# Attention projections: the transposes of normed query and key tiles stand five half-product steps behind their own product instead of four

## The chip, the cores and the metric

The kernel runs on one core of a Trainium2 chip. The metric is the time of one whole execution on the device, in microseconds (us). Engines are named as the profile names them: PE (TensorE; PEld is its weight load), DVE (VectorE), ACT (ScalarE), POOL (GpSimd), SP (SyncE, which issues most of the DMAs).

## What is computed

Two layers of a decoder with 16 meta tokens ahead of 512 tokens, width 1024. Layer 0 is attention with forget gates, layer 1 a gated recurrence; each is followed by a mixture-of-experts FFN. The change touches only the start of layer 0, where queries and keys are projected, normed for each head of 64 values, and laid out with the head dimension on the partitions:

```python
def fox_attention(h, w_in, b_f, g_q, g_k, w_out):
    q, k, v, f_logit = jnp.split(h @ w_in, [D_MODEL, 2 * D_MODEL, 3 * D_MODEL], axis=-1)
    q = rms_norm(q.reshape(bsz, length, FOX_HEADS, FOX_HEAD_DIM), g_q)
    k = rms_norm(k.reshape(bsz, length, FOX_HEADS, FOX_HEAD_DIM), g_k)
    v = v.reshape(bsz, length, FOX_HEADS, FOX_HEAD_DIM)
    ...  # softmax((q k^T) * scale + forget sums), times v, times w_out
```

## The kernel before

The projection goes by **chunks**: `q` first half, `k` first half, `q` second half, `k` second half, `v` first half, `v` second half (512 columns each; below q0, k0, q1, k1, v0, v1). A chunk has four **products**, one for each 128 tokens. A product is 24 matmuls of 128x512: weights and tokens are each split into a rounded part and a remainder (`whi`, `wlo`, `xhi`, `xlo`), and for each half of the weights come 8 matmuls with `whi` (L340 `pp<-whi,xhi` and `pp<-whi,xlo`) and 4 with `wlo`. The 16 meta rows have a product of their own, `pm` (L357, 8 matmuls), fed from the raw weights when a weight tile of the next chunk is split; that is after the first and after the last product of a chunk.

What follows a product of `q` or `k` is `heads_norm`, in three parts. At the product's end ACT squares it (L419 `sq`) and DVE sums by head (L421). The part `second` takes the root on ACT (L138, L139), refines it on DVE (L157 to L161) and scales the tile (L430 `qn<-pp,rs`). The part `third` transposes `qn` on PE (L438, four transposes into `pq`), and ACT copies `pq` into `qT` or `kT` with the gain (L439).

When the parts are issued is ruled by a counter, `Later`. It ticks twice in a product: after its 13th matmul (the **middle**) and at its end, behind `qk_post`, which calls `heads_norm`. A part put in with `later.at(n, f)` is issued at the n-th tick from then on:

```python
later.at(2, second)
later.at(4, third)
```

So `second` of a product stands in the middle of the next one. The engines' queues are in this order, each engine works its queue in order, and semaphores do the rest. A chunk's end is a busy place: behind the tick stands `W.split`, which feeds the meta product on PE, rounds the next weights on ACT (L280 `whi`) and takes the remainder on POOL or DVE or half on each (L295, L289 `wlo`). The meta rows pass through `heads_norm` too: the sums of their four partial products (L372 `mt`, and `vm` for `v`) and their `second` and `third` are put in with the same counter, in the middle of the next chunk's first product, so that their transposes (L438 from 16 rows) stand beside those of that chunk's first tile.

Buffers that bear on the order: `qn` has two, `sq` one, `pp` three, `pq` shares two PSUM banks with the transposes of the input, and `pm` shares two with small constants. During the chunks DVE also builds small masks (L857 to L867 `lmask`) as the iterator `later.slow`, one piece at each tick.

After the projections come the attention itself (L626 and on), the output projection with the router, and the experts of layer 0, whose weights begin to load when the attention's buffers close.

Of the kernel before, what the change touches and what calls it, by code (L numbers as in the profile page):

```python
# [127 lines left out]
def rsqrt(K, y, x, shape, pool, tag, tables):  # L128


    run(rsqrt_steps(K, y, x, shape, pool, tag, tables))
# [243 lines left out]
def fox(K):  # L375

    nc, tc = K.nc, K.tc
    later = Later()
    with tc.tile_pool(name="ax", bufs=1, reuse_waits="tile") as per:
# [15 lines left out]
        with tc.tile_pool(name="ap", bufs=1, reuse_waits="tile") as mid, \  # L395
# [20 lines left out]
            def heads_norm(src, r, dst, gcol, hp0, c0):  # L416

                sq = wk.tile([128, 512], FT, name="sq", bufs=1)
                nc.scalar.activation(sq[:r], src, AF.Square)  # L419
                ss = wk.tile([128, 8], FT, name="ss")  # L420
                nc.vector.tensor_reduce(ss[:r], sq[:r].rearrange("t (h d) -> t h d", d=HD), axis=AX.X, op=OP.add)  # L421
                nc.vector.tensor_scalar(ss[:r], ss[:r], 1.0 / HD, EPS, op0=OP.mult, op1=OP.add)
                held = []

                def second():
                    rs = wk.tile([128, 8], FT, name="rs")
                    qn = wk.tile([128, 512], FT, name="qn")
                    held.append(qn)
                    rsqrt(K, rs[:r], ss[:r], [r, 8], wk, "hn" if r == 128 else "hm", True)
                    nc.vector.tensor_tensor(qn[:r].rearrange("t (h d) -> t h d", d=HD),  # L430
                                            src.rearrange("t (h d) -> t h d", d=HD),
                                            rs[:r, :, None].to_broadcast([r, 8, HD]), op=OP.mult)

                def third():
                    qn, = held
                    p = ps.tile([128, 4, 128], FT, name="pq", tag="tr")
                    for a in range(4):
                        nc.tensor.transpose(p[:, a, :r], qn[:r, 128 * a:128 * a + 128], K.ident[:r, :r])  # L438
                    nc.scalar.activation(dst[:, hp0:hp0 + 4, c0:c0 + r], p[:, :, :r], AF.Copy, scale=gcol)  # L439

                later.at(2, second)
                later.at(4, third)

            def qk_post(p, i, kind, half):
                dst, gcol = (qT, gq) if kind == "q" else (kT, gk)
                heads_norm(p, 128, dst, gcol, 4 * half, M + 128 * i)

            def meta_done(mr, kind, half):
                if kind == "v":
                    mr.sum(vm[:, 512 * half:512 * half + 512])  # L450
                    return
                mt = wk.tile([M, 512], FT, name="mt", bufs=1)
                mr.sum(mt)
                dst, gcol = (qT, gq) if kind == "q" else (kT, gk)
                heads_norm(mt, M, dst, gcol, 4 * half, 0)
# [1636 lines left out]
```

## Time and profile before

| what | value |
|---|---|
| median of 3 runs | 1759.38 us (1757.03 to 1763.66) |
| the profiled execution, whole time | 1755.66 us |
| its span, first to last instruction | 1753.7 us |
| PE busy | 1617.5 us, 92% of the span |
| DVE, ACT, POOL busy | 758.1, 411.7, 280.3 us |
| mean granted clock of PE | 0.962 of full |

The projections take about the first tenth of the span, 9 to 190 us. PE is the engine that works nearly all the time there, so its idle time in that stretch, and time at a lower granted clock, are what to look for. The rows are quoted below, ahead of the prediction.

### The profile page before, as it was taken

To read this page: it belongs to the slowest core of one execution; us is meant where nothing else is said; L and a number is where in the kernel's file an instruction comes from. 1 tells how busy PE (TensorE), PEld (TensorE's weight loads), DVE (VectorE), ACT (ScalarE), POOL (GpSimd) and SP (SyncE) were. 2 spreads that over 40 slices of the span, in tenths; PEclk is the share of its full clock that TensorE was granted. 3 is DMA by queue.
4 is the path that set the end of the run, shared out by engine and by line. 5 is a ranking of instruction groups with operands and counts; after the bars stand their busy time and mean duration, and the time that the engine had idled before them with its cause. 6 is when DMAs were issued, how large, how long until landed. Compare 5 with 4: busy or idle time off the path is not lost. (4 is left out here: it accounts for less than half of the span.)

```text
span 1753.7 us, 23757 instructions
## 1 busy us (share of the span) xinstructions
PE 1617.5 (92%) x9397; PEld 877.0 (50%) x9397; DVE 758.1 (43%) x1832; ACT 411.7 (23%) x867; POOL 280.3 (16%) x385
## 2 busy tenths in 40 slices
PE   6998999986999999999979999998779999999998
PEld 4666766563343444343346777776533433333333
DVE  5664388353143433233452554564513334233334
ACT  5433256342000000000034323343301000000000
POOL 2423344100000000000023414434000000000000
PEclk9998989996999999999989999999889999999999
DMA  4222455436999999999941212124689999999996
GB/s 171 78 71 74 134 103 92 168 146 244 420 420 419 418 419 420 418 420 418 410 144 63 74 33 90 50 90 155 266 323 418 419 419 419 419 420 419 419 419 262
DMA packets 106695, 472.74 MB, mean 270 GB/s; under 512 B 16288, under 2 KB 34768, under 8 KB 58448
## 3 DMA queue, kind: packets, MB, share of 16 engines
q1 hardware_dynamic: 100096, 457.60, 66.7%
q0 software_dynamic: 5008, 8.76, 1.5%
q10 hardware_dynamic: 1472, 4.78, 0.7%
q8 instruction: 76, 1.25, 0.3%
q14 instruction: 43, 0.35, 0.1%
HBM read 472.97 MB, written 6.39 MB: 273 GB/s over the span
## 5 line engine op out<-in xcount | busy, mean ns | idle before, releaser
L1630 PE MATMUL pa<-w,hm 128*64 128x512 f32 x1024 | 236.5, 601 | 13.6 <-DMA w<-in_moe_w_up_dram 13.6
L1630 PE MATMUL pa<-w,xT 128*64 128x512 f32 x1024 | 234.7, 601 | 8.1 <-DMA w<-in_moe_w_up_dram 8.1
L1630 PE MATMUL py<-w,hT 128*64 128x512 f32 x960 | 226.7, 597 | 1.8 <-ACT hT L1674 1.5
L295 POOL TENSOR_TENSOR wlo<-w,whi 128x256 fp32r<-128x256 f32 x200 | 159.5, 836 | 359.8 <-ACT whi L280 234.6
L1697 DVE TENSOR_TENSOR h<-pc,h 128x512 f32<-128x512 f32 x256 | 160.3, 682 | 68.3 <-PE pc L313 68.2
L1426 POOL DMA_INDIRECT xg<-xd,row x32 | 32.1, 1002 | 852.2 <-PE pt L1609 696.9
L1630 PEld LDWEIGHTS pa<-w,hm 128*64 128x64 f32 x1024 | 74.7, 138 | 162.1 <-issue 132.3
L1630 PEld LDWEIGHTS pa<-w,xT 128*64 128x64 f32 x1024 | 76.8, 138 | 153.3 <-issue 129.3
L1630 PEld LDWEIGHTS py<-w,hT 128*64 128x64 f32 x960 | 68.9, 137 | 143.5 <-issue 128.9
L1614 DVE TENSOR_TENSOR hm<-pt,mg 128x512 f32<-128x512 f32 x32 | 22.1, 691 | 273.8 <-PE pt L1609 273.8
L1614 DVE TENSOR_TENSOR xT<-pt,mg 128x512 f32<-128x512 f32 x32 | 22.1, 691 | 269.0 <-PE pt L1609 269.0
L1661 ACT ACTIVATE sg<-pa 128x512 f32<-128x512 f32 x32 | 19.1, 597 | 468.7 <-PE pa L1630 468.7
L313 PE MATMUL pc<-yhi,OT 128*128 128x512 f32 x288 | 128.0, 444 | 1.2 <-DVE h L1697 1.2
L313 PE MATMUL pc<-ylo,OT 128*128 128x512 f32 x288 | 113.5, 394 | 0.0
L1674 ACT ACTIVATE hT<-pth 128x512 f32<-128x512 f32 x32 | 19.2, 599 | 316.7 <-PE pth L1672 316.7
L340 PE MATMUL pp<-whi,xhi 128*128 128x512 f32 x192 | 81.6, 425 | 2.1 <-ACT xhi L231 2.1
L340 PE MATMUL pp<-whi,xlo 128*128 128x512 f32 x192 | 81.9, 427 | 0.3 <-DVE xlo L233 0.2
L313 PEld LDWEIGHTS pc<-yhi,OT 128*128 128x128 f32 x288 | 52.3, 182 | 53.2 <-DVE h L1697 24.3
L897 PE MATMUL pp<-xhi,whi 128*128 128x512 f32 x168 | 70.5, 420 | 0.0
L897 PE MATMUL pp<-xlo,whi 128*128 128x512 f32 x168 | 66.6, 396 | 0.0
L280 ACT ACTIVATE whi<-w 128x2048 fp32r<-128x2048 f32 x32 | 60.8, 1909 | 0.1
L1686 ACT ACTIVATE yhi<-py,slot 128x512 fp32r<-128x512 f32 x64 | 42.1, 685 | 75.6 <-PE pc L313 62.0
(398 smaller groups left out, 2431.9 us busy)
## 6 DMA issues: line engine op xcount, KB each, us to landing
w<-in_moe_w_up_dram SPq DMA_DIRECT2D x256, 1024.0 KB, 19.9
w<-in_moe_w_down_dram SPq DMA_DIRECT2D x124, 1024.0 KB, 20.5
w<-in_hg_w_in_dram SPq DMA_DIRECT2D x16, 1024.0 KB, 5.3
w<-in_fox_w_in_dram SPq DMA_DIRECT2D x12, 1024.0 KB, 5.1
bias<-ncum SPq DMA_DIRECT2D x16, 264.0 KB, 4.2
w<-in_fox_w_out_dram SPq DMA_DIRECT2D x4, 1024.0 KB, 5.1
xd<-xn ACTq DMA_DIRECT2D x8, 512.0 KB, 2.7
w<-in_moe_w_down_dram SPq DMA_DIRECT2D x8, 512.0 KB, 12.0
```

The costliest lines, as they stand in the source:

```text
L280: nc.scalar.activation(hi, raw, AF.Copy)
L295: e.tensor_tensor(lo[at], raw[at], hi[at].bitcast(FT), op=OP.subtract)
L313: nc.tensor.matmul(p, a, b, start=(n == 0), stop=(n == len(terms) - 1))
L340: K.nc.tensor.matmul(p, a, b, start=(n == 0), stop=(n == len(ts) - 1))
L897: nc.tensor.matmul(p, a, b, start=(m == 0), stop=(m == len(terms) - 1))
L1426: K.nc.gpsimd.indirect_dma_start(x, None, K.xd[self.layer], bass.IndirectOffsetOnAxis(ap=row, axis=0), bounds_check=K.xd[self.layer].shape ...
L1614: nc.vector.tensor_tensor(xT[:, js], p[:, :, :n], gain[:, js, None].to_broadcast([128, 4, n]), op=OP.mult)
L1630: nc.tensor.matmul(p[c][64 * a:64 * a + 64], x[:, j, 64 * a:64 * a + 64], w[a][c], start=(j == 0), stop=(j == nj - 1), skip_group_check=Tr ...
L1661: nc.scalar.activation(sg[:n], pa[0][:n], AF.Sigmoid)
L1674: nc.scalar.activation(hT[:, :, :n], pt[:, :, :n], AF.Copy)
L1686: nc.scalar.activation(hi[:n], py[:n], AF.Copy, scale=g)
L1697: nc.vector.tensor_tensor(h[:, cs], p[:r], h[:, cs], op=OP.add)
```

## The change

`third` is put in one tick later: the four transposes of a normed tile stand at the end of the second product behind their own, instead of in its middle. `second` stays where it is. Nothing is added or removed.

```diff
                 later.at(2, second)
-                later.at(4, third)
+                later.at(5, third)
```

What the moved ticks do to the queues is seen in the order in which the built program's instructions stand. On PE, in the third product of chunk q1 (the same in k0 and k1), 16-row transposes of the meta tile and 128-row transposes of the chunk's first tile stand behind the 13th matmul before:

```order
L340 MATMUL pp<-whi,xhi 128x512
L438 MATMUL pq<-ident,qn 128x16 x4
L438 MATMUL pq<-ident,qn 128x128 x4
L340 MATMUL pp<-whi,xlo 128x512
L340 MATMUL pp<-whi,xhi 128x512
L340 MATMUL pp<-whi,xlo 128x512
L340 MATMUL pp<-whi,xhi 128x512
L340 MATMUL pp<-whi,xlo 128x512
L340 MATMUL pp<-whi,xhi 128x512
L340 MATMUL pp<-whi,xlo 128x512
L340 MATMUL pp<-wlo,xhi 128x512 x4
L340 MATMUL pp<-whi,xhi 128x512
```

After the change, at the same place on PE, they stand behind the product's last matmul:

```order
L340 MATMUL pp<-whi,xhi 128x512
L340 MATMUL pp<-whi,xlo 128x512
L340 MATMUL pp<-whi,xhi 128x512
L340 MATMUL pp<-whi,xlo 128x512
L340 MATMUL pp<-whi,xhi 128x512
L340 MATMUL pp<-whi,xlo 128x512
L340 MATMUL pp<-whi,xhi 128x512
L340 MATMUL pp<-whi,xlo 128x512
L340 MATMUL pp<-wlo,xhi 128x512 x4
L438 MATMUL pq<-ident,qn 128x16 x4
L438 MATMUL pq<-ident,qn 128x128 x4
L340 MATMUL pp<-whi,xhi 128x512
```

The two sets of transposes moved past eleven matmuls of their product. On ACT, at the end of chunk q1, the square of the last product is followed by the rounding of the next weights, and the copy of a transposed tile comes after it, before:

```order
L419 ACTIVATE sq<-pp 128x512
L280 ACTIVATE whi<-w 128x2048
L439 ACTIVATE qT<-pq,gq 128x4x128
L138 ACTIVATE hn_t<-ss 128x8
L139 ACTIVATE rs<-hn_t 128x8
L370 ACTIVATE mt<-pm 16x512
```

After the change, on ACT at the same chunk's end, the copy stands between the two:

```order
L419 ACTIVATE sq<-pp 128x512
L439 ACTIVATE qT<-pq,gq 128x4x128
L280 ACTIVATE whi<-w 128x2048
L138 ACTIVATE hn_t<-ss 128x8
L139 ACTIVATE rs<-hn_t 128x8
L370 ACTIVATE mt<-pm 16x512
```

The copy went ahead of the rounding and away from the root steps. The orders on DVE, POOL and SP are the same before and after.

## Rows read from the trace of the kernel before

**Rows 1.** The page: the span, PE's share, and the granted clock in 40 slices of the span (tenths).
```profile
span 1753.7 us, 23757 instructions
PE 1617.5 (92%) x9397; PEld 877.0 (50%) x9397; DVE 758.1 (43%) x1832; ACT 411.7 (23%) x867; POOL 280.3 (16%) x385
...
PEclk9998989996999999999989999999889999999999
```

**Rows 2.** What PE waited for from 0 to 220 us: who waited for whom, us in total, times, longest.
```profile
PE pq L438 <- DVE lmask L860: 2.4, 1, 2.4
PE pq L438 <- DVE lmask L866: 2.4, 1, 2.4
PE pm L357 <- issue: 2.2, 1, 2.2
...
PE pq L438 <- DVE xt L227: 1.5, 1, 1.5
...
PE pf L313 <- DVE wfl L580: 0.3, 1, 0.3
```

**Rows 3.** PE in order of time in chunk k0: start, duration, instruction, and in brackets the idle time before it. The 13th matmul of the third product, the first of the fourth, and the transposes behind that one's 13th.
```profile
79.97 0.39 PE L340 MATMUL pp<-whi,xhi 128*128 128x512 f32 x1
...
83.69 0.40 PE L340 MATMUL pp<-whi,xhi 128*128 128x512 f32 x1
...
86.72 0.60 PE L438 MATMUL pq<-ident,qn 128*128 128x128 f32 x4
```

**Rows 4.** PE in order of time in chunk q1: the same place, third to fourth product.
```profile
107.31 0.39 PE L340 MATMUL pp<-whi,xhi 128*128 128x512 f32 x1
...
110.44 1.09 PE L438 MATMUL pq<-ident,qn 128*128 128x128 f32 x4 [2.39 <-DVE lmask L860]
...
114.82 0.39 PE L340 MATMUL pp<-whi,xhi 128*128 128x512 f32 x1
```

**Rows 5.** PE in order of time in chunk k1: the same place again.
```profile
138.29 0.39 PE L340 MATMUL pp<-whi,xhi 128*128 128x512 f32 x1
...
147.35 0.47 PE L340 MATMUL pp<-whi,xhi 128*128 128x512 f32 x1
```

**Rows 6.** Busy time of each engine in three stretches, then the granted PE clock, DMA share and GB/s.
```profile
110.40:113.40 3.00, 2.96 (x9) 2.57 (x10) 1.99 (x11) 0.99 (x3) 0.00 (x0) 0.50 0.92 299
...
141.70:147.30 5.60, 5.53 (x15) 4.55 (x16) 3.05 (x12) 1.41 (x4) 0.00 (x0) 0.50 0.57 190
...
164.50:168.00 3.50, 3.50 (x13) 2.76 (x10) 0.00 (x0) 0.00 (x0) 3.50 (x6) 0.51 0.03 9
```

**Rows 7.** PE in order of time in chunk q0, the first tile's transposes in the middle of the third product.
```profile
45.44 0.66 PE L438 MATMUL pq<-ident,qn 128*128 128x128 f32 x4 [1.51 <-DVE xt L227]
```

**Rows 8.** DVE in order of time at the same place in q0: the last input tile with its gain, and its remainder.
```profile
44.71 1.27 DVE L227 TENSOR_TENSOR xt<-pt,gain 128x512 f32<-128x512 f32 x2
46.09 1.29 DVE L233 TENSOR_TENSOR xlo<-xt,xhi 128x512 fp32r<-128x512 f32 x2
```

**Rows 9.** DVE in order of time: the scaled first tile of q1 and of k1, and then, in chunk v0, half of the weights' remainder, the first refining step of the last key tile's root, and the sums of the meta rows of `v`.
```profile
109.60 0.69 DVE L430 TENSOR_TENSOR qn<-pp,rs 128x512 f32<-128x512 f32 x1
...
140.93 0.69 DVE L430 TENSOR_TENSOR qn<-pp,rs 128x512 f32<-128x512 f32 x1
...
156.08 1.22 DVE L289 TENSOR_TENSOR wlo<-w,whi 128x1024 fp32r<-128x1024 f32 x1 [0.81 <-ACT whi L280]
159.36 0.66 DVE L157 TENSOR_TENSOR hn_t<-rs 128x8 f32<-128x8 f32 x1 [2.06 <-ACT rs L139]
...
161.25 2.13 DVE L372 TENSOR_TENSOR vm<-pm,vm 16x512 f32<-16x512 f32 x3
```

**Rows 10.** PE in order of time in chunk v0: the meta feed behind its first product, the second product's first matmul, and the transposes behind that product's 13th.
```profile
163.48 1.05 PE L357 MATMUL pm<-w,xm 128*16 128x512 f32 x8 [2.24 <-issue]
164.47 0.71 PE L340 MATMUL pp<-whi,xhi 128*128 128x512 f32 x1
...
169.14 0.60 PE L438 MATMUL pq<-ident,qn 128*128 128x128 f32 x4
```

**Rows 11.** ACT in order of time: a copy of a transposed tile in k0 and the instruction behind it, and the rounding of weights at the end of q1.
```profile
87.36 0.69 ACT L439 ACTIVATE kT<-pq,gk 128x512 f32<-128x512 f32 x1 [2.87 <-PE pq L438]
87.94 0.20 ACT L138 ACTIVATE hn_t<-ss 128x8 f32<-128x8 f32 x1
...
121.55 1.91 ACT L280 ACTIVATE whi<-w 128x2048 fp32r<-128x2048 f32 x1
```

**Rows 12.** POOL in order of time: its half of the weights' remainder for k1 and for v0.
```profile
123.53 3.89 POOL L295 TENSOR_TENSOR wlo<-w,whi 128x256 fp32r<-128x256 f32 x4 [14.05 <-ACT whi L280]
...
156.13 3.88 POOL L295 TENSOR_TENSOR wlo<-w,whi 128x256 fp32r<-128x256 f32 x4 [15.33 <-ACT whi L280]
```

**Rows 13.** PE in order of time: the meta feed at the end of q1, and the four matmuls with that remainder in the first product of k1 and of v0.
```profile
120.94 1.05 PE L357 MATMUL pm<-w,xm 128*16 128x512 f32 x8
...
127.13 1.32 PE L340 MATMUL pp<-wlo,xhi 128*128 128x512 f32 x4
...
160.15 1.09 PE L340 MATMUL pp<-wlo,xhi 128*128 128x512 f32 x4
```

**Rows 14.** SP's queue from 230 to 460 us: what the issue of weight tiles (L81) waited for longest at the attention's end.
```profile
SPq L81 <- PE pom L777: 28.8, 1, 28.8
```

**Rows 15.** SP in order of time: the first loads of the experts' weights of layer 0.
```profile
325.36 79.20 SPq L81 DMA_DIRECT2D w<-in_moe_w_up_dram  x16
```

## Prediction

> **What bounds the kernel now.** I read the page first: PE is busy 92% of the span, and its granted clock is not full in every slice [rows 1]. The change touches only the projections, so the next view was the list of what PE waits for up to 220 us. Three rows name the transposes `pq`: twice 2.4 us put down to a mask instruction of DVE, once 1.5 us behind an input tile, and a fourth row is a meta feed `pm` with 2.2 us [rows 2]. The masks are only the DVE instruction that stood next in the queue; PE's order of time shows what is late: the scaled tile `qn` of the chunk's first product. In q1 it is written until 109.60 + 0.69 = 110.29 us, and PE starts its transposes at 110.44 after 2.39 us of idling [rows 4, 9].
>
> The wait is not the whole price. Chunk k0 has the same place without a wait: from the 13th matmul of the third product to the first of the fourth PE needs 83.69 - 79.97 = 3.72 us [rows 3]. q1 needs 114.82 - 107.31 = 7.51, which is 3.79 more; k1 needs 147.35 - 138.29 = 9.06, which is 5.34 more [rows 4, 5]. [...] The feed in v0 is the same story: 2.24 us of idling, then 0.51 from 164.5 to 168.0 [rows 6, 10]; its second product needs 169.14 - 164.47 = 4.67 us to its transposes, against 86.72 - 83.69 = 3.03 in k0 [rows 3, 10], so 1.64 for the clock.
>
> **The change, part by part.** Each of the 20 sets of four transposes moves from the middle of a product to its end, behind eleven matmuls. Their count, their length and the DMAs are the same; the DVE, POOL and SP queues keep their order. So the sum is made of waits that go, waits that come, and clock.
>
> *q0.* The transposes wait 1.51 us because their PSUM bank is still read by `xt` [rows 7]. Without the wait PE would be there at 43.93; eleven matmuls at 3.03 / 13 = 0.233 us bring it to 46.5, after the first of the two `xt` is done (about 45.35). The fourth product then starts some 1.4 us later, behind the transposes and the meta feed, and needs `xlo`, done at 47.38 [rows 8]: still hidden. Gain 1.51.
>
> *q1 and k1.* PE passes the middle at 107.31 + 0.23 and reaches the new place at 110.1, in k1 at 141.1. First come the meta tile's transposes, no longer than the 0.60 of a set in rows of k0 [rows 3], so the first tile's `qn` is wanted between 110.1 and 110.7, and 141.1 and 141.7. It is written until 110.29 and 141.62 [rows 4, 5, 9]: at worst 0.2 and 0.5 us of waiting are left with DVE as it is. DVE should be some 0.6 us earlier, since the root steps on ACT no longer stand behind a copy that takes 87.94 - 87.36 = 0.58 us [rows 11]. Gain 3.79 and 5.34, if the clock stays up too.
>
> *The waits that come.* `qn` has two buffers and at a chunk's start three tiles for them, so DVE may write the first tile of q1 only after the last tile of k0 is transposed. That was in the middle of the second product and is now at its end, about 104.5 (107.31 less twelve matmuls) + 0.6. DVE gets to it at 109.60 [rows 9], so there are over 4 us to spare; behind it on DVE stand the next tile's sum and masks, which then lose nothing.
>
> The wait that I do charge is on ACT. At a chunk's end the copy now stands ahead of the rounding `whi`, and it has to wait for the transposes. In k0 a copy starts 87.36 - 86.72 = 0.64 us after its transposes and takes 0.58 [rows 3, 11], so `whi` starts 1.22 us after PE begins what follows the product, where it now starts 121.55 - 120.94 = 0.61 after [rows 11, 13]: 0.61 late. Its readers are late by as much. In k1 POOL ends at 127.42 and PE already waits for it, 1.32 instead of 1.09 us [rows 12, 13]: all 0.61 shows. In k0 the forget-gate product waits 0.3 us for DVE behind the same weights [rows 2]: 0.61 more. In v0 POOL ends at 160.01 and the second of the four matmuls stands at 160.38 [rows 12, 13], so 0.24 of it shows, just ahead of the meta feed. k0 to q1 splits on DVE alone and has time. Bounds: nothing, if POOL is less disturbed, to three times 1.33 = 4.0 (a whole copy of 0.69 and its start).
>
> *The feed in v0.* It needs its PSUM bank, which DVE reads until 161.25 + 2.13 = 163.38 [rows 9]. The chain ahead is the root step at 159.36, which waited 2.06 us for ACT, and ACT was held by a key copy in the product's middle. That copy moves; DVE is then free after `wlo`, at 156.08 + 1.22 + 0.61 = 157.91, so the sums end 1.45 us earlier. PE, there at 161.24 + 0.24, waits about half a microsecond more instead of 2.24 [rows 10]. Gain 1.45 (the 0.24 is in it), and 1.64 of clock if so short a gap leaves it up. Bounds: 0 to 2.24, and 0 to 1.64.
>
> Sum: 1.51 + 3.79 + 5.34 + 1.45 + 1.64 - 0.61 - 0.61 = 12.5 us. It reaches the end: the first loads of the experts' weights come at 325.36, released by the attention's last matmuls on PE after 28.8 us of waiting [rows 14, 15], so that stage starts earlier by the same amount. The profiled execution took 1755.66 us, so 1743.2; the median of the runs, 1759.38, stands 3.7 above it, and I forecast 1747.
>
> [...]
>
> **Rivals.**
>
> *The clock is not given back.* The idling goes, but about as much time at half clock stays, since the half-microsecond gaps that remain or come are enough. For: 1.51 us in q0 and gaps of that kind exist, and the clock part is large, 3.79 - 2.39 + 5.34 - 2.39 + 1.64 = 6.0 of 12.5. Against: in k0 and most of the stretch PE runs at full clock. It gives a gain of 6.5, so 1753; with the waits at their upper bound some 4, so 1755.5.
>
> *The gain is lost later.* The attention or the router might wait for something that does not move, and the time stays 1759. Against: the loads of rows 14 are released by PE, so I see nothing fixed.
>
> *Slower: the copy holds the weights.* ACT works in order, so if the transposes at a chunk's end had to wait for their own `qn`, then copy, `whi`, `wlo` and the next product would all wait, and the clock would fall on top. Price at each of three chunk ends: the wait plus up to 2.95 of clock, the dearer of the two seen (5.34 - 2.39). Against the 13.7 gained elsewhere this turns to over 0.5% slower (8.8 us) only when the waits are (13.7 + 8.8) / 3 - 2.95 = 4.6 us each; then 1768 or more. The tile wanted there is the second of its chunk. DVE writes it one product after the first, so some 3 us after 110.29, and PE asks for it at the fourth product's end, 110.1 + 0.9 + 24 x 0.233 = 116.6: it would have to be about 8 us late in all.
>
> **How the numbers follow.** The forecast has 0.62 (its own range 1745 to 1751: gains of 8.8 to 14.5 taken from 1755.66, moved by up to 3.7), the clock rival 0.20, no gain 0.12, slower 0.06. About 0.5%, 8.8 us, is what a measurement of this kernel can tell from no change. Faster by more: 0.62 and a little of the clock rival, 0.64; same 0.30; slower 0.06. The range 1740 to 1757 takes in the largest sum (14.5, with no new wait and the whole 2.24, 1741.2) and the clock rival's end, with the spread of the runs.
>
> **What would show it.** In the trace after, the two waits of 2.39 on `pq` and the 1.51 in q0 are gone; the third to fourth product of q1 and k1 takes about 3.7 us; the granted clock stays at full from 100 to 150 us; `whi` starts 1.2 us behind a chunk's last product; the first product of k1 waits some 0.8 us for `wlo`; the feed in v0 waits half a microsecond; the first expert loads stand near 313. The prediction is wrong if the transposes wait at the products' ends, if a new stretch at half clock appears behind the `wlo` waits, or if the loads move by less than the projections do.

## The result and the profile after

The changed kernel took 1750.62 us (median of 6 runs, 1745.28 to 1752.94) beside 1759.34 us for the kernel before (6 runs, 1757.03 to 1764.39): a ratio of 0.9941 with an interval of [0.9917, 0.9966], 8.7 us less. With the runs that the experiments added, the two unedited kernels stand at 1746.5 us (13 runs, 1740.7 to 1752.94) and 1757.5 us (67 runs, 1748.34 to 1769.76; the six above are not among them, since their clock is not on record), 11.0 us apart. Forecast were 1747 us and a gain of 12.5.

The page of the changed kernel: span and granted clock of PE in 40 slices (lines of [rows 1]). PE is busy 1614.3 us.

```profile
span 1748.8 us, 23756 instructions
...
PEclk9999889996999999999989999999889999999999
```

What PE waited for up to 220 us, the list of [rows 2]. No row for `pq` is left; the feed in v0 fell from 2.2 to 0.9 us; the forget gate's waits and those for `wlo` grew.

```profile
PE pm L357 <- ACT kT L439: 0.9, 1, 0.9
PE pp L340 <- POOL wlo L295: 0.9, 2, 0.5
...
PE pf L313 <- DVE wfh L579: 0.4, 1, 0.4
PE pf L313 <- DVE wfl L580: 0.4, 1, 0.4
```

PE in order of time, the changed kernel. First q1's third product from its 13th matmul, the transposes (meta tile and first tile counted together) at its new place, and the first matmul of the fourth; then the end of q1 and the first product of k1 with its wait; k1's third to fourth product; and in v0 the 13th matmul of the first product, the feed, and the first matmul of the second product. These answer to [rows 4, 5, 10, 13].

```profile
106.70 0.39 PE L340 MATMUL pp<-whi,xhi 128*128 128x512 f32 x1
...
109.59 1.00 PE L438 MATMUL pq<-ident,qn 16*128 16x16 f32 x8
110.34 0.47 PE L340 MATMUL pp<-whi,xhi 128*128 128x512 f32 x1
...
116.01 0.60 PE L438 MATMUL pq<-ident,qn 128*128 128x128 f32 x4
...
123.19 0.96 PE L340 MATMUL pp<-wlo,xhi 128*128 128x512 f32 x3 [0.50 <-POOL wlo L295]
...
134.44 0.39 PE L340 MATMUL pp<-whi,xhi 128*128 128x512 f32 x1
...
138.08 0.47 PE L340 MATMUL pp<-whi,xhi 128*128 128x512 f32 x1
...
148.16 0.40 PE L340 MATMUL pp<-whi,xhi 128*128 128x512 f32 x1
...
153.26 1.05 PE L357 MATMUL pm<-w,xm 128*16 128x512 f32 x8 [0.92 <-ACT kT L439]
154.24 0.51 PE L340 MATMUL pp<-whi,xhi 128*128 128x512 f32 x1
```

From third to fourth product q1 now needs 110.34 - 106.70 = 3.64 us and k1 138.08 - 134.44 = 3.64, where [rows 4, 5] gave 7.51 and 9.06: 3.87 and 5.42 us less. The prediction put all that k1 needed beyond the 2.39 down to the clock. But PE also waited there for the meta tile's `qn`, a fourth row on `pq` that the list of before has and the prediction passed over:

```profile
138.99 0.39 PE L438 MATMUL pq<-ident,qn 16*128 16x16 f32 x4 [0.31 <-DVE qn L430]
```

That 0.31 is gone too.

The clock, in the windows of the changed kernel's profile (busy time of each engine, then the granted clock, DMA share and GB/s). It is full through q1, k1 and v0, where [rows 6] has three stretches at 0.50 and 0.51.

```profile
100.00:150.00 50.00, 49.50 (x241) 36.92 (x240) 38.31 (x97) 21.64 (x45) 19.09 (x23) 1.00 0.19 64
150.00:203.00 53.00, 49.93 (x223) 36.85 (x221) 12.19 (x34) 12.36 (x21) 18.53 (x27) 1.00 0.46 134
203.50:231.00 27.50, 25.84 (x137) 17.56 (x135) 21.92 (x67) 11.21 (x33) 12.39 (x20) 0.50 0.47 92
```

The third window is the start of the attention, and there the first comparison of profiles loses half of what it had won. PE begins its first score product (L313, `s`) at 195.87 us, 11.8 before the 207.64 of the kernel before. But the first loads of the experts' weights come at 319.41, against 325.36 in [rows 15]: only 6.0 earlier. In between, half clock was granted for 13.5 us at the attention's start before (216 to 229.5) and for 27.5 now.

```profile
319.41 12.62 SPq L81 DMA_DIRECT2D w<-in_moe_w_up_dram  x6
```

Two theories: A, where the clock falls in the attention differs from run to run in either kernel, and the change has no part in it; B, the change makes it, since its attention starts behind a different history of PE. The experiments begin there.

### The profile page after: what moved, and what is told of

It is laid out like the page before. It is cut to its first block, busy times and chain, and to the rows that moved or that the text cites. A ratio compares the mean times of both kernels' runs of the same rounds, so it can differ in the third digit from the quotient of the medians.

```text
span 1748.8 us, 23756 instructions
## 1 busy us (share of the span) xinstructions
PE 1614.3 (92%) x9397; PEld 872.9 (50%) x9397; DVE 762.3 (44%) x1832; ACT 411.0 (24%) x867; POOL 281.8 (16%) x385
## 5 line engine op out<-in xcount | busy, mean ns | idle before, releaser
L313 PE MATMUL pc<-yhi,OT 128*128 128x512 f32 x288 | 128.2, 445 | 1.2 <-DVE h L1697 1.2
L313 PE MATMUL pc<-ylo,OT 128*128 128x512 f32 x288 | 113.4, 394 | 0.0
L313 PEld LDWEIGHTS pc<-yhi,OT 128*128 128x128 f32 x288 | 52.3, 182 | 53.3 <-DVE h L1697 24.3
L340 PE MATMUL pp<-whi,xlo 128*128 128x512 f32 x192 | 78.2, 407 | 0.5 <-DVE xlo L233 0.5
## 6 DMA issues: line engine op xcount, KB each, us to landing
w<-in_moe_w_down_dram SPq DMA_DIRECT2D x124, 1024.0 KB, 20.5
```

The costliest lines, as they stand in the source:

```text
L313: nc.tensor.matmul(p, a, b, start=(n == 0), stop=(n == len(terms) - 1))
L340: K.nc.tensor.matmul(p, a, b, start=(n == 0), stop=(n == len(ts) - 1))
```

## The experiments

### Both kernels once more

No edit.

Changed kernel: 

> The changed kernel once more, unedited, for a second profile. In the first one the attention's first scores on PE stood at 195.9 us (207.6 before the change), 11.7 earlier, but the experts' first loads only 6.0 earlier (319.4 against 325.4): between them PE ran at half clock from 203.5 to 231 us, before the change from 216 to 229.5. Theory A, the length of that stretch is chance, and differs from run to run of one kernel: first scores again at 195.9 within 0.5 us, the half-clock stretch another length than 27.5 us by several us, and the loads earlier by about half of the difference. Theory B, the change itself makes the stretch long: again 27 us within 4, loads at 319.4 within 1.

Kernel before: 

> The kernel before once more, unedited, for a second profile. Theory A (chance): first scores near 207.6, the half-clock stretch at the attention's start another length than 13.5 us, possibly as long as 27. Theory B (made by the change): 13.5 within 4, loads at 325.4 within 1.

Measured: 1743.2 and 1765.72 us, 22.5 apart, with the same programs. Windows at the attention's start, first the changed kernel, then the kernel before:

```profile
206.50:220.00 13.50, 12.34 (x79) 9.35 (x78) 12.05 (x42) 6.71 (x20) 7.24 (x12) 0.50 0.41 99
```

```profile
110.00:115.00 5.00, 3.73 (x19) 3.13 (x20) 4.06 (x17) 1.50 (x4) 0.30 (x1) 1.00 0.65 213
140.00:147.00 7.00, 5.81 (x27) 4.82 (x28) 5.13 (x18) 1.89 (x5) 0.23 (x1) 1.00 0.45 152
160.50:164.00 3.50, 3.50 (x13) 1.65 (x6) 0.08 (x1) 0.00 (x0) 3.46 (x6) 0.51 0.21 80
...
211.50:249.00 37.50, 36.01 (x173) 24.68 (x173) 26.31 (x85) 15.21 (x44) 14.77 (x24) 0.50 0.40 83
```

The stretch is 13.5 us in the changed kernel and 37.5 in the kernel before, the reverse of the first pair. Theory B falls. The second fence holds more: in this run the kernel before kept the full clock through q1 and k1, although it idled there as ever. PE in order of time in that run's q1, from the 13th matmul of the third product to the first of the fourth:

```profile
108.16 0.39 PE L340 MATMUL pp<-whi,xhi 128*128 128x512 f32 x1
...
111.27 0.63 PE L438 MATMUL pq<-ident,qn 128*128 128x128 f32 x4 [2.37 <-DVE lmask L860]
...
114.29 0.40 PE L340 MATMUL pp<-whi,xhi 128*128 128x512 f32 x1
```

That is 114.29 - 108.16 = 6.13 us with a wait of 2.37 at full clock, against 7.51 with a wait of 2.39 in [rows 4]. So the 1.40 us that the prediction charged to the clock in q1 is there in one profile and gone in another.

### One profile more of the kernel before, and runs of the changed kernel

No edit.

Kernel before: 

> One more profile of the kernel before, for its clock between 100 and 170 us: two profiles so far, of which one shows half clock behind the waits of q1, k1 and v0 and the other behind v0's alone. Theory A: waits of 2.39 us at q1 and k1 as before, and half clock behind some of them or none. Theory B: half clock behind all three, as in the first profile.

Changed kernel: 

> The changed kernel again, unedited, beside many runs of the kernel before, to part the gain into its waits and its clock. Of the runs so far, 46 of the kernel before have a mean granted clock of 0.9616 and 7 of the changed kernel 0.9634; over all kernels a run's span falls by about 1.39 us for each 0.001 of its mean clock. Theory A (the 6.5 us of waits in the prediction's sum are right, its 6.0 us of clock are too many, since the clock falls at those waits in some runs only): time of the changed kernel 1746 to 1751, ratio 0.993 to 0.996; at equal mean clock the two kernels stand 6 to 8 us apart, and the mean clock differs by 0.001 to 0.003, worth 1.5 to 4 us. Theory B (the sum was right in full and the first six runs fell low by chance): median 1744 to 1746, ratio 0.992 or less, clocks apart by 0.004. Theory C (a gain of 4 us at most): ratio 0.997 or more.

The third profile of the kernel before (1755.07 us) has the two waits on `pq` at 2.38 and 2.39 us, and in its windows full clock behind q1's and half clock behind k1's and behind the feed in v0:

```profile
110.00:115.00 5.00, 3.96 (x20) 3.32 (x21) 3.94 (x18) 1.59 (x4) 0.07 (x1) 1.00 0.65 213
140.00:146.50 6.50, 5.53 (x15) 4.55 (x16) 3.85 (x14) 1.41 (x4) 0.01 (x1) 0.50 0.47 164
163.50:167.00 3.50, 3.50 (x12) 2.71 (x9) 0.00 (x0) 0.00 (x0) 3.50 (x6) 0.53 0.03 12
```

The changed kernel stood at 1745.58 us (6 runs) beside 1758.52 (20 runs), ratio 0.9916 [0.9885, 0.9948], 12.9 us. Taken alone, these runs meet Theory B: the mean clocks are 0.965 and 0.9611, and the ratio is under 0.992. But in the first comparison the changed kernel's six runs had 0.9632, so six runs are too few for the clock, and all runs have to be taken. The 155 runs of both kernels and of the edits below, fitted with one level for each kernel and one slope, give 1.41 us (standard error 0.07) for each 0.001 of mean granted clock. At 0.964 the kernel before takes 1755.1 us and the changed one 1747.4: 7.7 apart (standard error 0.7). The mean clocks over all runs are 0.9615 and 0.9642, worth 3.8 us (standard error 0.8, from the scatter of the clocks). Together 11.5, the difference of the means. That is Theory A's split for the whole set, with the part at equal clock, which Theory A takes for the waits, at its upper end, and the total (standard error 1.1) not far enough from 12.5 to exclude it.

The profiles say the same in their own units (all of them unedited, half clock read in steps of 0.5 us):

| kernel | first score product | half clock, 100 us to there | first expert loads | half clock between | us between | from the loads to the end |
|---|---|---|---|---|---|---|
| before | 207.6 | 14.0 | 325.4 | 20.5 | 117.7 | 1428.3 |
| before | 204.5 | 3.5 | 332.4 | 44.5 | 128.0 | 1431.2 |
| before | 206.8 | 10.0 | 324.6 | 20.5 | 117.8 | 1428.5 |
| changed | 195.9 | 0 | 319.4 | 33.9 | 123.5 | 1429.4 |
| changed | 198.2 | 0 | 313.2 | 13.5 | 115.0 | 1428.0 |
| changed | 196.8 | 0 | 316.4 | 24.0 | 119.7 | 1428.1 |

From scores to loads the time follows the half clock: 109.6 us plus 0.41 us for each us of it meets these six and the six profiles of edits without added work, none of them off by more than 0.9. Behind the loads the six differ by at most 3.2 us.

### The first tile of a chunk alone, and all the others alone

The meta tile and each chunk's first tile one tick later, the others as before; and the other way round, with 4 and 5 exchanged. The first of the two edits, against the changed kernel:

```diff
-            def heads_norm(src, r, dst, gcol, hp0, c0):
+            def heads_norm(src, r, dst, gcol, hp0, c0, n=4):
 ...
-                later.at(5, third)
+                later.at(n, third)
 ...
-                heads_norm(p, 128, dst, gcol, 4 * half, M + 128 * i)
+                heads_norm(p, 128, dst, gcol, 4 * half, M + 128 * i, 5 if i == 0 else 4)
 ...
-                heads_norm(mt, M, dst, gcol, 4 * half, 0)
+                heads_norm(mt, M, dst, gcol, 4 * half, 0, 5)
```

First tiles: 

> One part alone: the transposes of the meta tile and of each chunk's first tile five steps behind, those of the other three tiles four as before. If the gain is the three waits of PE on the first tile (1.51 in q0, 2.39 in q1, 2.39 in k1) and the clock they cost, nearly all of it is here: those waits gone, the rounding of the weights in its old place ahead of the copy, so no longer waits for the weights' remainder, and the meta feed in v0 still waiting some 2.2 us; first scores of the attention 7 to 10 us earlier than the 204.5 to 207.6 of the two profiles of the kernel before: 196 to 199.5. The whole time 1747 to 1752, the attention's own clock being chance. If the gain is spread over all tiles, first scores stay above 201.

Others: 

> The other part alone: meta and first tiles four steps behind as before, the other three tiles five. By my theory the waits of 2.39 in q1 and k1 stay, the copy moves ahead of the rounding (about half a microsecond more waiting for weights in k0, k1 and v0 each) and the feed in v0 gets about 1.4 us shorter: first scores within 1.5 us of the kernel before (203 to 208), whole time the same as before, 1752 to 1762. If the gain is spread over all tiles, it gains 5 us or more here too.

Measured: 1749.09 us, ratio 0.9967 [0.9944, 0.9991], and 1750.58 us, ratio 0.9953 [0.993, 0.9976], beside 1757.09. The medians and the ratios order the two differently, so neither order is shown. The second was expected at no change and gained 6.5 us in the medians. At equal mean clock (0.964) they stand 4.9 and 2.6 us below the kernel before (standard error 0.8 each).

With the others alone, the waits of q1 and k1 are 1.38 and 1.14 us instead of 2.39, though their own transposes have not moved. What moved is a copy one chunk earlier. PE's 13th matmul in q1's first product, the copy of k0's third tile on ACT, and the first refining step of k0's last tile on DVE, before:

```profile
94.06 0.40 PE L340 MATMUL pp<-whi,xhi 128*128 128x512 f32 x1
...
94.94 0.69 ACT L439 ACTIVATE kT<-pq,gk 128x512 f32<-128x512 f32 x1 [2.63 <-PE pq L438]
...
96.00 0.17 DVE L157 TENSOR_TENSOR hn_t<-rs 128x8 f32<-128x8 f32 x1 [1.36 <-ACT rs L139]
```

With the others alone, the same matmul, the root step of k0's last tile and the copy of k0's third tile on ACT, then DVE as far as the scaled first tile of q1, and PE's wait for it:

```profile
95.39 0.40 PE L340 MATMUL pp<-whi,xhi 128*128 128x512 f32 x1
...
94.24 0.21 ACT L139 ACTIVATE rs<-hn_t 128x8 f32<-128x8 f32 x1
...
101.83 0.68 ACT L439 ACTIVATE kT<-pq,gk 128x512 f32<-128x512 f32 x1
...
94.14 2.29 DVE L289 TENSOR_TENSOR wlo<-w,whi 128x2048 fp32r<-128x2048 f32 x1 [1.76 <-ACT whi L280]
96.35 0.16 DVE L157 TENSOR_TENSOR hn_t<-rs 128x8 f32<-128x8 f32 x1
...
109.91 0.69 DVE L430 TENSOR_TENSOR qn<-pp,rs 128x512 f32<-128x512 f32 x1
...
110.75 0.63 PE L438 MATMUL pq<-ident,qn 128*128 128x128 f32 x4 [1.38 <-DVE lmask L860]
```

Before, the copy in the middle of q1's first product waited for its transposes, the root steps of k0's last tile stood behind it, and DVE idled 1.36 us. With the copy gone from there, DVE goes on right behind `wlo`, and that step starts 96.35 - 95.39 = 0.96 us behind PE's 13th matmul instead of 96.00 - 94.06 = 1.94. From that step DVE needs as long as before to the first tile's `qn`, by way of the meta rows: 109.91 - 96.35 = 13.56 us, against 109.60 - 96.00 = 13.60 [rows 9]. So `qn` is 1.0 us earlier beside PE's matmuls, which is what the wait lost. A chunk's end helps the next chunk's start.

With the first tiles alone, the wait list has the feed in v0 unchanged and a new wait on `pq` in k1:

```profile
PE pm L357 <- issue: 2.2, 1, 2.2
PE pq L438 <- ACT kT L439: 1.0, 1, 1.0
```

By the traces, with 0.31 for the meta tile's wait in k1, which both versions lose, and 0.96 for the feed, which the others alone win: first tiles 1.51 + 2 x 2.39 + 0.31 - 0.22 (left in k1) - 1.01 = 5.4; others (2.39 - 1.38) + (2.39 - 1.14) + 0.31 + 0.96, less 0.6 at the forget gate and 0.5 for `wlo`, 2.4. Both lie within the standard error of the 4.9 and 2.6 measured. That these add up to 7.5, beside the changed kernel's 7.7, is in part chance: both versions take from the same waits in q1 and k1, and the first adds one of its own.

### One tick more, and the weights ahead of the copy

All `third` steps at 6 instead of 5:

```diff
-                later.at(5, third)
+                later.at(6, third)
```

Six: 

> All transposes six steps behind instead of five, that is again in a product's middle, one product later than before the change. If five steps already hide every wait on the tiles, nothing more is won there: first scores within 1.5 us of the changed kernel (195 to 199.5), the rounding back in its old place, the feed in v0 waiting about 2 us again. The two buffers of the tiles are now held for two products; if DVE is stopped by them for as long as a product, transposes wait again and first scores stand above 200.

Measured: 1747.62 us (10 runs), ratio 0.9933 [0.9909, 0.9958]; at equal clock 1747.8, the changed kernel's 1747.4. No wait on `pq` was left to be won, and the feed in v0 is back at 2.47 us, with half clock behind it:

```profile
154.75 1.71 PE L357 MATMUL pm<-w,xm 128*16 128x512 f32 x8 [2.47 <-ACT whi L280]
```

```profile
155.00:158.50 3.50, 3.50 (x13) 1.73 (x6) 0.54 (x1) 0.00 (x0) 3.50 (x6) 0.51 0.17 64
```

The other edit leaves 5 and puts the rounding of the next weights ahead of the tick at a chunk's end, so that ACT rounds before it copies:

```diff
-                    later.tick()
+                    if i < NT - 1 or not nxt:
+                        later.tick()
 ...
                     W.split(*([nc.vector] if busy else [nc.gpsimd, nc.vector]), first=lambda raw: mr.feed(raw, 4))
+                    later.tick()
```

Rounding first: 

> The changed kernel, and at a chunk's end the next weights' rounding is issued ahead of the tick, so that on ACT it stands ahead of the copy again, as before the change (on PE the meta feed then stands ahead of the transposes). If the late rounding costs what I charged, 0.6 us in k0 and in k1, the waits for the remainder go back to those of the kernel before (0.2 to 0.4) and first scores stand about 1.2 us earlier than in the changed kernel with the same clock, 194 to 197. If the charge was wrong, the waits and the first scores stay as in the changed kernel, 195.9 to 198.2.

Again, with more runs: 

> The changed kernel with the rounding of the next weights put ahead of the moved copy at a chunk's end, again, since only four runs of it stand so far (median 1744.15). If that order is worth something by itself: 2 us or more below the changed kernel in this call, at equal mean clock too. If its four runs were lucky: within 1.5 us of the changed kernel. The trace of its first profile speaks for little: its first product of the v0 stage waited 1.49 us for the copy where the changed kernel's waited 0.92, and its first scores stood at 195.4 us as against 195.9.

Both edits: 

> Both at once: third steps six products behind and the rounding ahead of the copy at a chunk's end. With six alone the v0 stage's first product waits 2.47 us for the rounding of the weights; with that rounding ahead the wait should fall to about 1 us. If the gains add up: 1.5 us or more below six products alone, which stood at 1747.6, so 1743 to 1746. If nothing past five steps is left to be gained: within 1.5 us of the changed kernel.

Rounding first took 1744.15 us (4 runs), then 1747.25 (9 runs, ratio 0.9934 [0.9908, 0.996]), where the changed kernel beside it took 1745.58: the four were lucky. Over all 13 it stands at 1746.6, and at equal clock 0.9 us below the changed kernel with a standard error of 0.9, which tells nothing. Its wait list does answer the question that it was built for. The late rounding's price in k0 and k1 is gone: of the waits for `wlo` only v1's is left, and the forget gate is back at 0.4 us in all, where the changed kernel has 0.9 and 0.7.

```profile
PE pp L340 <- POOL wlo L295: 0.4, 1, 0.4
```

The feed in v0 waits longer in exchange, 1.49 us instead of 0.92.

Both edits together took 1748.56 us (ratio 0.9943 [0.9921, 0.9966]). The wait of 2.47 did not fall to 1 us as expected: I had read it by its name, the rounding `whi`. DVE in the same two profiles shows what it was, the sums of the meta rows that hold the feed's PSUM bank. First six, then both:

```profile
152.51 2.13 DVE L372 TENSOR_TENSOR vm<-pm,vm 16x512 f32<-16x512 f32 x3
```

```profile
152.02 2.13 DVE L372 TENSOR_TENSOR vm<-pm,vm 16x512 f32<-16x512 f32 x3
```

They end at 154.64 and 154.15; the feeds start at 154.75 and 154.25, both after 2.47 us. None of these versions is shown to beat the changed kernel.

### Added matmuls at the attention's start

Can denser work on PE keep the clock up there? 24 products 128x128x512 into an unused PSUM bank, spread over the scores of heads 2 to 4, in both kernels:

```diff
+        extra = {2: 3, 3: 2, 4: 1}
 ...
+                for _ in range(extra.get(hd, 0)):
+                    nc.tensor.matmul(junk, QK[hp][0][0][:, :128], QK[hp][1][0][:, :512], start=True, stop=True)
```

Changed kernel: 

> The changed kernel with 24 extra dense matmuls of 128x128 by 128x512 in the scores of heads 2 to 4, written to a PSUM bank that nothing reads; they cost about 0.23 us each at full clock, 5.6 us, less what falls in PE's idle time. If the lost gain is the clock at the attention's start (theories A and B both), the half-clock stretch there shrinks to under 10 us and the time from first scores to the experts' first loads is 118 or less, against 123.5 in the changed kernel, so 1746 to 1751 in all. If something else holds that stretch (a wait on DVE, ACT or POOL), it stays near 27 us or the time grows by the 5.6 us, to 1756.

Kernel before: 

> The kernel before with the same 24 extra matmuls. If the clock at the attention's start is all that hid the gain, this one and the changed one with the same matmuls differ by what the projections gain, 11.7 us, plus or minus 3, and the half-clock stretches there are alike: 1757 to 1763. If the change costs the attention something else, they differ by 9 or less.

Measured: 1756.65 us, ratio 0.9981 [0.9956, 1.0005], and 1766.63 us, ratio 1.0043 [1.0018, 1.0069], some 10 us more each and above both forecasts for a spared clock, 1746 to 1751 and 1757 to 1763. The changed kernel's windows:

```profile
203.50:213.50 10.00, 10.00 (x28) 6.29 (x27) 4.02 (x16) 1.98 (x8) 3.73 (x7) 0.50 0.35 88
217.00:227.50 10.50, 10.50 (x32) 6.75 (x32) 7.18 (x26) 3.72 (x12) 1.88 (x4) 0.51 0.26 60
```

PE is busy all of these 20.5 us at half clock. In the kernel before the stretch was 27.5 us, so the added work did not spare it. Both numbers lie within the 13.5 to 37.5 seen without it, and whether it shifts the average stays open. The pair repeats the main result: 10.0 us apart in the medians, 7.3 at equal clock.

## Why the prediction was right, and where a term was off

The time came out as forecast: 1750.6 in the first comparison, 1746.5 over all runs, where 1747 was said. Part of that is luck. The 1747 takes 12.5 from 1759.4, the median of three runs; over its 67 runs the kernel before stands 1.9 lower, and the gain is 11.0, so two misses cancel.

Of the 12.5 us, 6.5 were waits. The traces give 1.51 (q0) + 2 x 2.39 (q1, k1) + 0.31 (the meta tile in k1) + 0.96 (the feed) - 0.57 (the forget gate) - 0.54 (`wlo` in k1) = 6.5 as well, with parts off in both directions, and the runs at equal clock 7.7 (standard error 0.7); whether the 1.2 between these two is more than scatter stays open. The other 6.0 were clock, of which 0.31 was the meta tile's wait in k1; measured are 3.8 (standard error 0.8).

*q0.* Gain 1.51: the wait is gone.

*q1 and k1.* The waits of 2.39 are gone and nothing is left in their place; the third to fourth product takes 3.64 us where some 3.7 was said. PE comes later by eleven matmuls, which alone is enough in q1: the kernel with the first tiles alone has no wait there, and 0.22 in k1. DVE is earlier besides, by 1.0 us and not 0.6, as the kernel with the other tiles alone shows. The reason given was right in kind, a copy that no longer stands ahead of root steps. But it is the copy of the third tile of the chunk before, and with it went its wait for the transposes.

*The waits that come.* `whi` was to start 1.22 us after PE begins what follows the product. At the end of q1 the transposes start at 116.01 and ACT's rows in order of time are

```profile
116.70 0.68 ACT L439 ACTIVATE qT<-pq,gq 128x512 f32<-128x512 f32 x1
117.28 1.91 ACT L280 ACTIVATE whi<-w 128x2048 fp32r<-128x2048 f32 x1
```

so 1.27. In k1 PE waits 0.50 for `wlo` in a gap of its own, where 0.8 was named; from the 13th matmul of k1's first product to the second product it needs 125.50 - 120.43 = 5.07 us instead of 129.36 - 124.83 = 4.53, 0.54 more (0.61 charged). At the forget gate the list has 0.36 + 0.35 where [rows 2] has 0.3 in all, and k0's first product, the forget gate with it, takes 0.57 us longer by PE's order of time (0.61 charged). That both hang on the late rounding is shown by the version that rounds first.

*The feed in v0.* The sums on DVE were to run back to back behind `wlo` and to end 1.45 us earlier. They do run without a gap, but DVE's second refining step took 0.67 us instead of 0.17. First the kernel before, with the 13th matmul of v0's first product, then the changed one:

```profile
157.43 0.40 PE L340 MATMUL pp<-whi,xhi 128*128 128x512 f32 x1
...
160.06 0.17 DVE L159 SCALAR_TENSOR_TENSOR hn_t<-hn_t,ss 128x8 f32<-128x8 f32 x1
```

```profile
146.95 1.23 DVE L289 TENSOR_TENSOR wlo<-w,whi 128x1024 fp32r<-128x1024 f32 x1 [1.15 <-ACT whi L280]
148.10 0.70 DVE L157 TENSOR_TENSOR hn_t<-rs 128x8 f32<-128x8 f32 x1
148.84 0.67 DVE L159 SCALAR_TENSOR_TENSOR hn_t<-hn_t,ss 128x8 f32<-128x8 f32 x1
...
151.03 2.13 DVE L372 TENSOR_TENSOR vm<-pm,vm 16x512 f32<-16x512 f32 x3
```

The third step took 0.66 instead of 0.17. Before, these two ran after POOL's half of `wlo` had ended at 160.01 [rows 12]; now they run beside it (147.00 to 150.88). From the first step to the sums DVE needs 2.93 us instead of 1.89, so the sums end at 153.16, 5.00 us behind PE's 13th matmul (148.16) instead of 5.95, and the feed starts at 153.26. From that matmul to the second product PE needs 154.24 - 148.16 = 6.08 us instead of 164.47 - 157.43 = 7.04 [rows 10]: the gain is 0.96 of the 1.45, and 0.92 of waiting is left, not half a microsecond. That it hangs on a copy in the product's middle is shown by the first tiles alone, which leave that copy in place and the 2.2 us with it.

*The clock.* This is the term that was mis-sized. The 1.40 in q1 and the 2.95 in k1 that the sum counts as clock stand on one profile alone, where 0.50 was granted over 3.0 and 5.6 us [rows 6], each right behind a wait of 2.39. I took that profile's stretches as the kernel's, and no other profile shows as much. With the profile that had the added matmuls later on, four profiles show the kernel before from q1 to v0: 14.0, 3.5, 10.0 and 10.5 us at half clock, 9.5 on the mean, and the one I had was the largest. At 0.41 us for each, as between scores and loads, 9.5 are by estimate 3.9 us, against the 3.8 that the runs' clocks give; and half clock for 9.5 of 1755 us lowers the mean clock by 0.0027, which is what the runs' mean clocks differ by. The change does take these away: in the four such profiles of the changed code no half clock falls between 100 us and the first scores. The clock changes fall differently from run to run of one program: in q1 the same wait, 2.37 to 2.4 us, was followed by half clock in two of these four profiles and not in two. The prediction's rival, that about as much half clock would stay, is not what happened: 3.8 us came back on the mean.

*It reaches the end.* I named the loads near 313 us, and said that the prediction fails if they move by less than the projections do. In the first pair they did, 6.0 against 11.8. No wait took the rest: the loads came at 319.4, 313.2 and 316.4 in three profiles, following the half clock in between, which ran from 13.5 to 33.9 us in the changed kernel and from 20.5 to 44.5 in the kernel before. Over many runs the mean clocks show no such loss, over one pair it can hide half of the gain.

*Slower: the copy holds the weights.* No transposes wait at a chunk's end; the mechanism is visible only in `whi`, which is 1.27 - 0.61 = 0.66 us later.

## What to carry to other kernels

Price a stall in two terms: the idle time, which one profile gives to a tenth of a microsecond (2.37 to 2.39 in q1 in the three profiles without added work), and the clock behind it, which needs several profiles because it comes and goes with the same program (in q1 there in one of those three). When two kernels differ by under 1%, regress the time of all runs on their mean granted clock: the levels then tell the two kernels apart at one clock, the clock's share stands beside them, and a lucky set of four runs shows as what it is. A wait's named releaser need not be what was waited for (the 2.47 us put down to `whi` ended 0.1 us behind the sums on DVE); look for the instruction whose end coincides with the start. When a wait shrinks in a version that did not touch it, follow the late tile back through its engines to the first place where it is late against PE.

## What the runs showed of the hardware

- A wait of 2.37 to 2.4 us on PE was followed by a granted clock of 0.50 in some runs and not in others (q1: two of four profiles; k1: three of four). Behind the feed in v0 a wait of 2.2 to 2.5 us was followed by it in all seven profiles that have one, and waits of 0.9 to 1.5 us there never (seven profiles).
- At the attention's start the clock fell to half in every profile, for 13.5, 17 to 17.5, 27 to 27.5 or 37.5 us in versions without added work, though PE was busy for 88 to 96% of it (12.34 of 13.5 and 36.01 of 37.5 us in the fences above). What decides the length is open. I did not try to change the order of the attention's work itself.
- A microsecond at half clock costs 0.41 us there, by the line through twelve profiles. The spread of the runs is mostly clock: the kernel before has a standard deviation of 4.5 us (21 from lowest to highest), and 2.2 are left at equal clock.
- The refining steps of a 128x8 tile on DVE (L157 to L161) took 0.17 us at most where POOL was not at work on a `wlo` (67 steps), and 0.65 to 0.81 in 28 of the 29 steps that began while it was, in one trace of each kernel up to 200 us. In q1 before the change all three steps ahead of the first tile's `qn` took that long (0.70, 0.65 and 0.65 us), which by estimate is 1.5 of the 2.39 us of PE's wait. No version was run with POOL's work elsewhere, so this is read from the order in time alone.
